# Reading and writing the columns of a matmul in other orders, in two feed-forward groups of a two-layer encoder

## The chip, the cores and the metric

The kernel runs on one core of a Trainium2 chip. The metric is the device time of one execution in microseconds. The kernel before takes 1174.57 us, the median of three runs (1173.69 to 1175.23).

## What is computed

Two layers act on x, 512 tokens by 1024 features. Each has an attention part (eight stick-breaking heads and four differential ones, with a common input and output projection) and a feed-forward part. In outline, with the attention left out:

```
for l in range(2):
    h = rmsnorm(x, attn_norm[l])
    x = x + attention(h @ w_in[l]) @ w_o[l]
    h = rmsnorm(x, mlp_norm[l])
    u = square(relu(h @ w_ff1[l]))      # 1024 -> 4096
    x = x + u @ w_ff2[l]                # 4096 -> 1024
return rmsnorm(x, final_norm)
```

The change lies in the product `h @ w_ff1[0]`.

## The kernel before

Activations lie transposed in SBUF: features on the 128 partitions, the 512 tokens along the free dimension. `h` has eight chunks of 128 features (`KC = 8`), held as two tiles, `h_hi` and `h_lo` ([128, 8, 512]): the value rounded to fp32r, and the remainder. Weights are split in the same way into `whi` and `wlo`, by one ScalarE copy (L116) and one VectorE subtraction (L117). A product is then three matmuls into the same PSUM bank, `hi x hi`, `hi x lo` and `lo x hi`; the helper `three` (L278) issues them at L281 to L283. In each the weight block of 128 x 128 is the stationary operand, and 512 columns of the other operand are the moving one. The output is one PSUM bank, 128 x 512 in fp32, so that column t of the moving operand gives column t of the bank.

The generator `block` (L291) computes 128 features of a projection for all tokens. It asks for a bank, takes the next weight unit, and issues `three` for each of the eight chunks in turn, 24 matmuls in all; the first opens the accumulation (`start`) and the last closes it (`stop`). `hpair(c)` gives the two halves of chunk c of `h`, `wpair(u, c)` those of the weights. Attention uses `block` for its projections, with names that begin with p; the feed-forward part uses it with names of the form `f{layer}_{group}_{k}`.

The feed-forward part works in four groups (`GROUPS = 4`), each of 1024 hidden features. A group has two halves. First come eight blocks (`2 * GP = 8`) of the first matrix. As each block ends, `evict_u` (L800) reads the bank: ScalarE takes the relu (L810) and squares it (L811), and sums and differences of the results are split into the tiles `Ah` and `Al` (L224, L225). Then the second matrix is multiplied in seven combinations of its quarters (`FORMS`, seven products in place of eight), which also go through `three`; their banks are gathered into `y` by ScalarE (L833) or VectorE (L835).

No order is written out by hand around the change: the framework places the instructions of each engine, and their order follows the program text. The weight unit after the next is split while the present one is used (`next`, L142), and while a group is computed its quarters of the second matrix are loaded and summed by DMA (`grow`, L783). In attention the projections are interleaved with scores (L465, L466), transposes of the attention weights (L555) and products with v (L583, L584; 256 columns each) by a budget of costs; this happens before the feed-forward part of the layer and has no bearing on the order within it. The v tiles are written by ScalarE at L381, in one of two layouts: for one head group in pieces of 64 columns, for the other in pieces of 128.

Of the kernel before, what the change touches and what calls it, by code (L numbers as in the profile page):

```python
# [22 lines left out]
KC = D // P  # L23
# [62 lines left out]
class _Weights:  # L86
# [55 lines left out]
    def next(self, kind):  # L142
        i = self.used
        assert _UNITS[i][0] in kind
        self.used += 1
        if i > 0:
            self.do_split(i + 2 * len(self.pools), i)
        return self.tiles.pop(i)
# [3 lines left out]
def trunk(ctx, tc, xT, w, w2, gains, gfin, lamv, cos, sin, out):  # L152
    nc = tc.nc
# [8 lines left out]
    def bank(tag, name):  # L162
        if tag == "any":
            tag = ("mm", "s", "s", "mm", "s")[turn[0] % 5]
            turn[0] += 1
        return ps.tile([P, 512], F32, tag=tag, name=name, bufs=banks[tag])
# [111 lines left out]
    def three(pt, a, b, first, last):  # L278
        ah, al = a
        bh, bl = b  # L280
        nc.tensor.matmul(pt, ah, bh, start=first, stop=False)  # L281
        nc.tensor.matmul(pt, ah, bl, start=False, stop=False)  # L282
        nc.tensor.matmul(pt, al, bh, start=False, stop=last)  # L283

    def hpair(c):
        return h_hi[:, c, :], h_lo[:, c, :]

    def wpair(u, c, n=P):
        return u[0][:, c * n : (c + 1) * n], u[1][:, c * n : (c + 1) * n]

    def block(name, tag="mm"):  # L291
        pt = bank(tag, name)
        u = W.next("px" if name[0] == "p" else "1")
        for c in range(KC):
            three(pt, wpair(u, c), hpair(c), c == 0, c == KC - 1)
            yield pt if c == KC - 1 else None

    def constants(a2):
# [18 lines left out]
    for l in range(L):  # L317
        with ExitStack() as actx:
# [379 lines left out]
            def dense():  # L698
                pts = opened_by.pop() if l else None
                if l == 0:  # L700
                    us = [W.next("x"), W.next("x")]
                    pts = [bank("mm", f"p{l}{i}") for i in range(2)]
                    turns = [(c, i) for c in range(5) for i in range(2)] + [(c, i) for i in range(2) for c in (5, 6, 7)]
                    for c, i in turns:
                        three(pts[i], wpair(us[i], c), hpair(c), c == 0, c == KC - 1)
                        yield 3 * 0.216
                step, b = 2 * KC, int(ORDER[0][1])
                held = [(pts[0], "d", b, "q"), (pts[1], "d", b, "k")]
                for item in ORDER[1:]:
                    kind, b = item[0], int(item[1])  # L710
                    for which in ("qk" if kind in "ds" else "v"):
                        name = f"p{l}{kind}{b}{which}"
                        for pt in block(name, "s" if step in (16, 24, 32) else "mm"):
                            step += 1
                            if step == RA[l]:
                                dgs["a"] = rms_a(ssq, 1.0 / D, rcol, f"a{l}", nc.vector, tr)
                            if step == RB[l]:
                                rms_b(rbc, f"a{l}", dgs["a"])
                                nc.vector.tensor_mul(cos_t, cos_t, rbc)
                                nc.vector.tensor_mul(sin_t, sin_t, rbc)  # L720
                            yield 3 * 0.216
                        held.append((pt, kind, b, which))
                        if step >= RB[l]:
                            for args in held:
                                {"w": evict_v, "u": evict_v, "s": evict_s, "d": evict_d}[args[1]](*args)
                            held = []
                yield from wo(1)
# [5 lines left out]
            for cost in dense():  # L733
# [5 lines left out]
                while live and credit > 0:  # L739
                    c = next(at, None)  # L740
# [17 lines left out]
        with ExitStack() as fctx:  # L758
            fp = fctx.enter_context(tc.tile_pool(name=f"ff{l}", bufs=1))
            f2 = fctx.enter_context(tc.tile_pool(name=f"f2{l}", bufs=2))  # L760
            last = l == L - 1
# [149 lines left out]
            for g in range(GROUPS):  # L911
# [12 lines left out]
                for k in range(2 * GP):  # L924
                    for n, pt in enumerate(block(f"f{l}_{g}_{k}", "any")):
                        if (g, k, n) == (0, 0, 6):
                            ptr = bank("t", f"rs_m{l}")
                            for j in range(4):
                                nc.tensor.transpose(ptr[:, j * P : (j + 1) * P], ssq[:, j * P : (j + 1) * P], ident)
                            nc.vector.tensor_reduce(  # L930
                                out=r2, in_=ptr.rearrange("p (j f) -> p j f", j=4), axis=AX.X, op=ALU.add)
                            nc.vector.tensor_scalar(
                                out=r2, in0=r2, scalar1=1.0 / D, scalar2=EPS, op0=ALU.mult, op1=ALU.add)
                            nc.vector.reciprocal(r2, r2)
                    evict_u(pt, g, k, forms)
                    if end and k in (2, 3):
                        settle(k - 2, 0)
                for f, form in enumerate(FORMS):
# [6 lines left out]
                    for n, (c, i, r) in enumerate(work):  # L945
                        if c not in held:
                            held[c] = W.next("f")
                        u = held[c]
# [65 lines left out]
            if last:  # L1014
                add_to(1, 0, to[1])
                square(1, 0)
                store(0, 0, False)
                weigh(0, 1)
                store(0, 1, True)
                weigh(1, 1, nc.gpsimd)  # L1020
                root(1)
                store(1, 0, False)
                store(1, 1, True)
            else:
                W.pools.pop()
                us = [W.next("x"), W.next("x")]
                pts = [bank("mm", f"p{l + 1}{i}") for i in range(2)]
                for tb in (0, 1):
                    add_to(tb, 0, to[tb])
                for c in CAME[2:4]:  # L1030
                    back(c)
                for n, c in enumerate(CAME):
                    if n in (2, 3):
                        for c_ in (CAME[4:6], CAME[6:])[n - 2]:
                            h = back(c_)
                    for i in range(2):
                        three(pts[i], wpair(us[i], c), hpair(c), n == 0, c == CAME[-1])
                squares = [add_sq(c, n == 0, ft, nc.vector) for n, c in enumerate(CAME)]
                for n in (0, 1):
                    behind(squares[n][n], h[n])  # L1040
                for p, q in zip(squares[1:], squares):
                    behind(p[0], q[0])
                opened_by.append(pts)
# [66 lines left out]
```

## Time and profile before

| | |
|---|---|
| median of three runs | 1174.57 us |
| span of the profiled execution | 1173.7 us |
| PE busy, share of the span | 1149.1 us, 98% |
| DVE busy, ACT busy | 817.8 us (70%), 651.7 us (56%) |
| share of PE in the chain that ended last | 84% |
| group 1 of layer 0, its eight blocks | 331.40 to 374.92 us |
| group 2 of layer 0, its eight blocks | 413.00 to 456.52 us |

The span is the time from the first to the last instruction of one profiled execution. PE is TensorE's matrix multiplication and PEld its weight loads, which run beside it; DVE is VectorE, ACT ScalarE, POOL GpSimd and SP the engine that issues most DMAs. In a row of the timeline stand the start, the duration (both in us), the engine, the line, the operation and its tiles, `out<-in`. `f` is the bank of a feed-forward block; names that begin with a number or `x`, such as `11010`, are banks of the seven combinations. A row of waits reads: who waited, for whom, us in total, how often, the longest.

### The profile page before, as it was taken

The numbers are of one execution on the slowest core, as the hardware profiler recorded it, in microseconds if no ns is written. First come the engines' busy times: TensorE is split into PE (matmuls) and PEld (weight loads), VectorE is DVE, ScalarE is ACT, GpSimd is POOL, SyncE is SP. The second block draws the span as 40 slices with busy tenths as digits, with TensorE's granted clock in tenths as the row PEclk, the third lists the DMA queues.
The fourth block names the chain that finished last, engine by engine and source line by source line (L and its number), as shares of the span: only waits on it lengthen the run. The fifth ranks groups of instructions, "written<-read, shape, count | busy, mean of one in ns | idle before, by whom it ended". The sixth has DMA issues, their size and how long they took to land.

```text
span 1173.7 us, 15335 instructions
## 1 busy us (share of the span) xinstructions
PE 1149.1 (98%) x5454; PEld 952.0 (81%) x5454; DVE 817.8 (70%) x1301; ACT 651.7 (56%) x1153; POOL 213.7 (18%) x283
## 2 busy tenths in 40 slices
PE   9999999999999999999899999999999999999995
PEld 6887888888888888888677888888888888888884
DVE  7888788785546747646878887877665466476567
ACT  6455666556656456455445556655666563554545
POOL 1221442130101101002012215331201010010022
PEclk9999999999999999999999999999999999999999
DMA  7645433245844836737416553432558357276184
GB/s 245 174 138 170 127 108 111 70 179 163 210 139 113 220 126 125 223 94 160 100 55 189 153 161 108 129 105 72 220 122 231 122 124 222 97 172 192 33 170 129
DMA packets 56860, 170.11 MB, mean 145 GB/s; under 512 B 7120, under 2 KB 8144, under 8 KB 56784
## 3 DMA queue, kind: packets, MB, share of 16 engines
q1 hardware_dynamic: 46416, 131.88, 33.7%
q0 software_dynamic: 10224, 37.23, 17.9%
q8 instruction: 43, 0.70, 0.2%
q14 instruction: 33, 0.27, 0.1%
q10 hardware_dynamic: 144, 0.02, 0.0%
HBM read 138.17 MB, written 2.10 MB: 120 GB/s over the span
## 4 chain that ended last, share of the span: by engine, by line
PE 84%; DVE 6%; DMA 3%; issue 2%; ACT 1%; POOL 1%; SPq 0%; POOLq 0%; DVEq 0%; ACTq 0%
PE f L282 10%; PE f L281 10%; PE f L283 10%; PE x L282 4%; PE x L281 4%; PE x L283 4%; PE wo L281 2%; PE wo L282 2%; PE wo L283 2%; DMA q<-in_w 2%; DVE wlo L117 1%; PE T0s L555 1%; PE T1s L555 1%; ACT whi L116 1%; DVE h_lo L229 1%
## 5 line engine op out<-in xcount | busy, mean ns | idle before, releaser
L117 DVE TENSOR_TENSOR wlo<-raw,whi 128x1024 fp32r<-128x1024 f32 (+1 forms) x132 | 158.0, 1201 | 95.9 <-ACT whi L116 95.0
L117 DVE TENSOR_TENSOR wlo<-q,whi 128x512 fp32r<-128x512 f32 x224 | 146.2, 688 | 106.0 <-ACT whi L116 105.6
L281 PE MATMUL f<-h_hi,whi 128*128 128x512 f32 x512 | 199.6, 390 | 0.0
L283 PE MATMUL f<-h_hi,wlo 128*128 128x512 f32 x512 | 199.2, 389 | 0.0
L282 PE MATMUL f<-h_lo,whi 128*128 128x512 f32 x512 | 199.2, 389 | 0.0
L116 ACT ACTIVATE whi<-q 128x512 fp32r<-128x512 f32 x224 | 129.5, 624 | 120.1 <-DMA q<-in_w 39.1
L116 ACT ACTIVATE whi<-raw 128x1024 fp32r<-128x1024 f32 (+1 forms) x132 | 133.9, 1019 | 111.0 <-PE f L282 54.5
L783 POOL DMA_DIRECT2D q<-in_w x64 | 55.9, 873 | 556.8 <-DVE wlo L117 471.4
L283 PEld LDWEIGHTS f<-h_hi,wlo 128*128 128x128 f32 x512 | 96.1, 188 | 20.0
L281 PEld LDWEIGHTS f<-h_hi,whi 128*128 128x128 f32 x512 | 96.1, 188 | 19.9
L282 PEld LDWEIGHTS f<-h_lo,whi 128*128 128x128 f32 x512 | 96.1, 188 | 19.7
L225 DVE TENSOR_TENSOR Al<-F,Ah 128x256 fp32r<-128x256 f32 (+2 forms) x96 | 74.8, 779 | 44.1 <-ACT Ah L224 44.0
L281 PE MATMUL x<-whi,Ah 128*128 128x512 f32 x256 | 100.2, 392 | 0.0
L282 PE MATMUL x<-wlo,Ah 128*128 128x512 f32 x256 | 99.7, 390 | 0.0
L283 PE MATMUL x<-whi,Al 128*128 128x512 f32 x256 | 99.7, 389 | 0.0
L224 ACT ACTIVATE Ah<-F 128x256 fp32r<-128x256 f32 (+2 forms) x96 | 67.6, 704 | 45.7 <-DVE F L819 43.7
L282 PEld LDWEIGHTS x<-wlo,Ah 128*128 128x128 f32 x256 | 48.1, 188 | 10.0 <-DVE wlo L117 0.4
L283 PEld LDWEIGHTS x<-whi,Al 128*128 128x128 f32 x256 | 48.0, 188 | 10.0
L281 PEld LDWEIGHTS x<-whi,Ah 128*128 128x128 f32 x256 | 48.1, 188 | 9.8
L810 ACT ACTIVATE F<-f 128x512 f32<-128x512 f32 x64 | 37.5, 587 | 9.9 <-DVE Al L225 5.5
L811 ACT ACTIVATE F<-F 128x512 f32<-128x512 f32 x64 | 40.3, 630 | 1.5
L228 ACT ACTIVATE h_hi<-x,g_all 128x512 fp32r<-128x512 f32 x32 | 22.6, 720 | 30.6 <-DVE x L692 17.5
(1060 smaller groups left out, 2574.6 us busy)
## 6 DMA issues: line engine op xcount, KB each, us to landing
raw<-in_w SPq DMA_DIRECT2D x126, 512.0 KB, 3.6
q<-in_w SPq DMA_DIRECT2D x64, 512.0 KB, 5.3
q<-in_w POOLq DMA_DIRECT2D x64, 512.0 KB, 5.7
x<-in_xT SPq DMA_DIRECT2D x8, 256.0 KB, 4.1
raw<-in_w SPq DMA_DIRECT2D x8, 128.0 KB, 4.1
yx<-y POOLq DMA_DIRECT2D x2, 512.0 KB, 8.8
y<-y POOLq DMA_DIRECT2D x2, 512.0 KB, 7.5
y<-yx POOLq DMA_DIRECT2D x2, 512.0 KB, 5.2
```

What stands on the lines that cost most here:

```text
L116: h = nc.scalar.activation(hi[:, a:b], raw[:, a:b], AF.Copy)
L117: self.last = h, nc.vector.tensor_tensor(out=lo[:, a:b], in0=raw[:, a:b], in1=hi[:, a:b].bitcast(F32), op=ALU.subtract)
L224: nc.scalar.activation(hi, src, AF.Copy)
L225: nc.vector.tensor_tensor(out=lo, in0=src, in1=hi.bitcast(F32), op=ALU.subtract)
L228: a = nc.scalar.activation(h_hi[:, c, :], x[:, c, :], AF.Copy, scale=g)
L281: nc.tensor.matmul(pt, ah, bh, start=first, stop=False)
L282: nc.tensor.matmul(pt, ah, bl, start=False, stop=False)
L283: nc.tensor.matmul(pt, al, bh, start=False, stop=last)
L555: nc.tensor.transpose(pt[:, off : off + P], u["w"][qi][:, kb * P : (kb + 1) * P], ident)
L783: nc.gpsimd.dma_start(t, quad(g, q, c), accum_op=ALU.add)
L810: nc.scalar.activation(t, pt, AF.Relu)
L811: nc.scalar.activation(t, t, AF.Square)
```

## The change

A table `READS` names an order for each of the eight chunks. `None` is the plain order, columns 0 to 511. A pair (n, b) cuts the 512 columns into n equal streams and takes b neighbouring columns of each stream in turn: with (2, 16) columns 0 to 15, 256 to 271, 16 to 31, 272 to 287, and so on. The same rearranged view is put on the moving operand and on the PSUM bank, so that each column's result lands where it did before. `three_by` is `three` with that view. `block` calls it for every projection, but with an order other than the plain one only where the name begins with `f0_1` or `f0_2`: groups 1 and 2 of layer 0, eight blocks each. The second matrix, attention and all other groups keep the plain order. Later lines move down by 17.

```
--- before.py
+++ after.py
@@ -282,6 +282,23 @@
         nc.tensor.matmul(pt, ah, bl, start=False, stop=False)
         nc.tensor.matmul(pt, al, bh, start=False, stop=last)
 
+    READS = (None, (2, 16), (2, 8), (2, 4), (2, 32), (4, 16), (2, 2), (8, 16))
+
+    def turns(c):
+        def view(t):
+            if READS[c] is None:
+                return t
+            n, b = READS[c]
+            return t.rearrange("p (n a b) -> p a n b", n=n, b=b)
+        return view
+
+    def three_by(pt, a, b, first, last, view):
+        ah, al = a
+        bh, bl = b
+        nc.tensor.matmul(view(pt), ah, view(bh), start=first, stop=False)
+        nc.tensor.matmul(view(pt), ah, view(bl), start=False, stop=False)
+        nc.tensor.matmul(view(pt), al, view(bh), start=False, stop=last)
+
     def hpair(c):
         return h_hi[:, c, :], h_lo[:, c, :]
 
@@ -292,7 +309,7 @@
         pt = bank(tag, name)
         u = W.next("px" if name[0] == "p" else "1")
         for c in range(KC):
-            three(pt, wpair(u, c), hpair(c), c == 0, c == KC - 1)
+            three_by(pt, wpair(u, c), hpair(c), c == 0, c == KC - 1, turns(c if name[:4] in ("f0_1", "f0_2") else 0))
             yield pt if c == KC - 1 else None
```

## The prediction

> **What bounds the kernel now.** I read the profile page first, its busy shares and its chain of waits.
>
> ```profile
> span 1173.7 us, 15335 instructions
> ## 1 busy us (share of the span) xinstructions
> PE 1149.1 (98%) x5454; PEld 952.0 (81%) x5454; DVE 817.8 (70%) x1301; ACT 651.7 (56%) x1153; POOL 213.7 (18%) x283
> ...
> PE 84%; DVE 6%; DMA 3%; issue 2%; ACT 1%; POOL 1%; SPq 0%; POOLq 0%; DVEq 0%; ACTq 0%
> PE f L282 10%; PE f L281 10%; PE f L283 10%; PE x L282 4%; PE x L281 4%; PE x L283 4%; PE wo L281 2%; PE wo L282 2%; PE wo L283 2%; DMA q<-in_w 2%; DVE wlo L117 1%; PE T0s L555 1%; PE T1s L555 1%; ACT whi L116 1%; DVE h_lo L229 1%
> ```
>
> TensorE carries 84% of the chain, and the three matmul lines that the change touches head the list. A 98% busy PE need not run at its best rate, so the stretches in question decide. From the timeline of PE I took where the two edited groups begin and end, and asked for the busy time of each engine in those two stretches and the one between them; first the f matmuls alone, then everything.
>
> ```profile
> 331.40:374.92 43.52, 43.52 (x192) 35.85 (x191) 4.11 (x7) 1.00 0.39 111
> 413.00:456.52 43.52, 43.52 (x192) 35.85 (x191) 4.10 (x7) 1.00 0.38 110
> ```
> ```profile
> 331.40:374.92 43.52, 43.52 (x193) 36.04 (x192) 21.26 (x30) 24.08 (x38) 1.73 (x2) 1.00 0.39 111
> 413.00:456.52 43.52, 43.52 (x193) 36.04 (x192) 22.25 (x32) 23.49 (x36) 1.72 (x2) 1.00 0.38 110
> ```
>
> The columns are the stretch, PE, weight loads, then (second fence) DVE, ACT and POOL, the granted clock, the DMA share and GB/s. In each stretch 192 matmuls fill 43.52 us without a gap: 43.52 / 192 = 226.7 ns from one start to the next. The clock is granted in full, 1.00. The timeline at the end of the first stretch shows the same beat one by one: three steps from 374.24 to 374.92 are 0.68 us.
>
> ```profile
> 374.24 0.39 PE L281 MATMUL f<-h_hi,whi 128*128 128x512 f32 x1
> 374.47 0.39 PE L282 MATMUL f<-h_lo,whi 128*128 128x512 f32 x1
> 374.70 0.39 PE L283 MATMUL f<-h_hi,wlo 128*128 128x512 f32 x1
> 374.92 0.39 PE L281 MATMUL 11010_3748<-whi,Ah 128*128 128x512 f32 x1
> ```
>
> The 0.39 us is the record of one matmul, with a modelled end; consecutive ones overlap, so the price of a matmul is the 226.7 ns between starts. Last, the waits between 331 and 457 us. Thirteen rows came back, and none begins with PE:
>
> ```profile
> POOL q L783 <- DVE wlo L117: 114.8, 7, 46.0
> DVE wlo L117 <- ACT whi L116: 40.4, 22, 4.0
> ACT whi L116 <- PE f L282: 27.4, 10, 4.2
> ...
> POOL q L783 <- issue: 0.2, 1, 0.2
> ```
>
> So PE never waits in this region, while ACT waits for PE. DVE (21 to 22 us of 43.52) and ACT (24 us) are about half idle. Whatever a reordered matmul costs or saves is paid one for one in the end time: there is no PE gap to hide it, and none that it could close.
>
> **The change part by part.** Nothing is removed, added or moved: 192 + 192 matmuls, the same weights, the same 512 columns, the same banks, the same buffers, DMAs and waits. What differs is the order in which 7 of the 8 chunks walk the columns. Each of the 16 blocks has three matmuls a chunk, so each order is run by 16 x 3 = 48 matmuls and the seven orders by 336; chunk 0 keeps its order. A walk is cut into runs of b neighbouring columns: 512 / b of them, that is 32, 64, 128, 16, 32, 256 and 32 for chunks 1 to 7, 560 in all, so 48 x 560 = 26,880 runs where there were 336.
>
> *The matmul itself.* No PE instruction of this trace reads or writes in pieces, so I bound the cost. Below: how much of the 226.7 ns does not grow with the columns? The 256-column matmuls tell.
>
> ```profile
> 207.74 0.28 PE L583 MATMUL O0s<-fh0s,vs 128*128 128x256 f32 x1
> 207.85 0.28 PE L584 MATMUL O0s<-fl0s,vs 128*128 128x256 f32 x1
> 207.97 0.28 PE L583 MATMUL O0s<-fh0s,vs 128*128 128x256 f32 x1
> 208.09 0.28 PE L584 MATMUL O0s<-fl0s,vs 128*128 128x256 f32 x1
> 208.21 0.40 PE L281 MATMUL wo<-mdh,whi 128*128 128x512 f32 x1
> ```
>
> Four steps from 207.74 to 208.21 are 0.47 us, 117.5 ns each. A column is (226.7 - 117.5) / 256 = 0.427 ns, so 512 of them are 218.4 ns and 8.3 ns are left over for each matmul. Every matmul pays the per-column part; an order could save at most the 8.3 ns. That is the lower end: 336 x 8.3 ns = 2.8 us gained.
>
> Above: the slowest column rate of a warm PE in this trace is that of the transposes.
>
> ```profile
> 205.79 0.49 PE L555 MATMUL T0s<-edge,sig0s 128*128 128x128 f32 x3
> ```
> ```profile
> L555 PE MATMUL T0s<-edge,sig0s x80: 270/272/301, 134.6 to 220.3; 128*128 128x128 f32 x80
> ```
>
> Three of them take 0.49 us to the last one's end, and one alone has a record of 0.27, so the two steps are 0.22 us: about 109 ns for 128 columns, 0.85 ns a column. A 512-column matmul at that rate would be 435 ns, 208 ns more than now. Taking it as the upper end, the cost of one order is between -0.4 us and 48 x 0.208 = 10.0 us, and of all seven between -2.8 us and 69.9 us.
>
> Between ends so far apart I go by the nearest row with a cut-up access. ScalarE has it: L381 writes the v tiles of one attention group as eight runs of 64 columns, those of the other as four runs of 128, and L224 writes `fh` in one run of 512, all from a PSUM bank.
>
> ```profile
> L381 ACT ACTIVATE vs<-vT0u x4: 597/602/610, 120.1 to 197.2; 128x512 fp32r<-128x512 f32 x4
> ```
> ```profile
> L381 ACT ACTIVATE vdh<-vT0w x4: 578/598/599, 37.6 to 94.7; 128x512 fp32r<-128x512 f32 x4
> ```
> ```profile
> L224 ACT ACTIVATE fh0s<-T0s x8: 597/600/607, 146.3 to 220.0; 128x512 fp32r<-128x512 f32 x8
> ```
>
> 602, 598 and 600 ns: a jump at the end of a run costs that engine nothing that can be seen. It is another engine, at a slower column rate and on the SBUF side; but it is an address walk of the same kind, and I take 0 for the matmul too. Both ends stay for the range.
>
> *Partial sums.* All three matmuls of a chunk use one order and each element is still added to once per matmul. From one chunk to the next the orders differ, so an element can come up again after fewer than 512 columns. Laying the walks end to end, the shortest return is 162 columns, from chunk 6 to chunk 7, or 162 x 0.427 = 69 ns; at all other borders it is 258 or more. In the rows above, 256-column matmuls of one accumulation return to an element every 117.5 ns without a stall; 69 ns is not shown. It would concern one border a block, 16 in all, and even 208 ns at each are 3.3 us; I price it at 0.
>
> *Weight loads and readers.* Each weight load has to fit beside a matmul: 35.85 / 191 = 188 ns of 226.7, so 39 ns are free and reordered matmuls can only lengthen that cover. ACT reads a bank when the last matmul of its block has ended, in its old order; its tile and its wait are the same.
>
> Sum: 1173.7 us of span plus 0. The three timed runs have a median of 1174.57 (1173.69 to 1175.23), 0.9 above the span of the profiled execution, so I forecast 1174.6. About 0.2%, 2.3 us, is what a measurement of this kernel can tell from no change.
>
> The rows cannot say how the memories that PE reads and writes treat a run of a given length. [...]
>
> **The rivals.**
>
> *Only the shortest runs cost.* Chunk 6 walks two streams in runs of two. Its reads change place 256 times a matmul, twice as often as chunk 3's. If the memory behind PE delivers in pieces longer than two columns, PE waits in chunk 6 alone. Price: at the transposes' rate 48 x 0.208 = 10.0 us, 1184.6: slower, against my forecast. It decides the verdict from 2.3 us / 48 = 48 ns a matmul. For it: each column now has only 0.427 ns, so there is no room for a second access. Against it: seven orders, and only one so short. 0.16.
>
> *Every run end costs.* If the address walk loses one column's time at each end of a run, in any order, that is 26,880 x 0.427 ns = 11.5 us, 1186.1; at two columns' time 1197.6. For it: PE walks a column in 0.427 ns where ScalarE takes 600 / 512 = 1.17 ns, fixed cost included, so it has less time to turn. Against it: the ScalarE rows, where seven further run ends cost 2 ns. 0.12, of which a little over half for one column's time.
>
> *Any order but the plain one is slow.* All 336 at the transposes' rate: 69.9 us, 1244.5. For it: no matmul of this trace is cut up, so no row excludes it. [...]
>
> *Faster.* Were the 8.3 ns a conflict between a matmul's first columns and the one before it, another order could dissolve it: at most 2.8 us, 1171.8. Against it: every matmul, in any order, still starts at column 0 and ends at 511, where a conflict between neighbours would lie. 0.03.
>
> **How the numbers follow.** The four rivals hold 0.40 and scatter and others 0.03. No change has 0.57. Slower by over 0.2%: 0.16 + 0.12 + 0.09 and 0.02 of the rest, 0.39. Faster by over 0.2%: 0.04. Predicted is the likeliest, 1174.6. The range goes from 1171.8, all 8.3 ns saved, to 1187.0, just past the short-run case and one column's time per run end: 0.57 + 0.16 + 0.07 + 0.02, about 0.82. Not in it are slow matmuls in all orders and run ends of two columns' time or more.
>
> **What would show it.** The two stretches of 192 f matmuls should again be 43.52 us; layer 1 has the same groups in the plain order and is the measure beside them. Within a block the 24 starts should be 226.7 ns apart throughout. If steps 19 to 21 of each block alone are longer, the first rival holds; if the excess goes as 32, 64, 128, 16, 32, 256, 32, the second; if chunks 1 to 7 are all long and alike, the third; steps of 218 ns would be the fourth. I am wrong if the two stretches differ from 43.52 by more than 1.2 us each, and wrong in kind if the time shows up elsewhere, such as a wait of PE within the region.

## The result, and the profile after

The changed kernel takes 1183.03 us, the median of three runs (1182.60 to 1186.01), against 1174.57 before: a ratio of 1.0079 with a 95% interval of 1.0057 to 1.0100. It is slower by 8.5 us. The forecast was no change; the range held the time, and what the likeliest case said of the matmuls was wrong.

The page of the changed kernel, in the parts shown of the one before:

```profile
span 1184.2 us, 15335 instructions
## 1 busy us (share of the span) xinstructions
PE 1159.4 (98%) x5454; PEld 953.4 (81%) x5454; DVE 818.3 (69%) x1301; ACT 652.1 (55%) x1153; POOL 214.1 (18%) x283
...
PE 84%; DVE 6%; issue 2%; DMA 2%; ACT 2%; POOL 1%; SPq 0%; POOLq 0%; ACTq 0%; DVEq 0%
```

The instructions are as many as before on every engine. PE is busy for 10.3 us more, and the span is 10.5 us longer; the other engines do the same work. Where the time lies is seen in the two stretches of 192 f matmuls (columns: stretch, PE, weight loads, ACT, granted clock, DMA share, GB/s):

```profile
331.82:380.12 48.30, 48.30 (x192) 36.31 (x191) 4.06 (x7) 1.00 0.38 102
418.22:466.52 48.30, 48.30 (x192) 36.31 (x191) 4.06 (x7) 1.00 0.36 98
```

Each is 48.30 us where it was 43.52: 4.78 us more, 9.6 us together, at the same clock. The profiled run was the slowest of the three, and the 0.9 us by which the span differs further lie inside the 3.4 us by which these runs differ. The waits between 331 and 467 us still have no row that begins with PE:

```profile
POOL q L800 <- DVE wlo L117: 123.7, 8, 48.4
DVE wlo L117 <- ACT whi L116: 48.2, 24, 4.6
ACT whi L116 <- PE f L299: 38.6, 16, 4.7
...
ACT whi L116 <- PE 11011_3749 L283: 0.2, 1, 0.2
```

The others wait longer for PE (ACT 38.6 us where it was 27.4, in a window 10 us longer); the time is inside the matmuls. The timeline of PE shows which. These are chunks 5, 6 and 7 of one block, and the first matmul of the next:

```profile
353.52 0.40 PE L298 MATMUL f<-h_hi,whi 128*128 128x512 f32 x1
353.76 0.40 PE L299 MATMUL f<-h_lo,whi 128*128 128x512 f32 x1
353.99 0.40 PE L300 MATMUL f<-h_hi,wlo 128*128 128x512 f32 x1
354.23 0.51 PE L298 MATMUL f<-h_hi,whi 128*128 128x512 f32 x1
354.56 0.51 PE L299 MATMUL f<-h_lo,whi 128*128 128x512 f32 x1
354.90 0.51 PE L300 MATMUL f<-h_hi,wlo 128*128 128x512 f32 x1
355.24 0.41 PE L298 MATMUL f<-h_hi,whi 128*128 128x512 f32 x1
355.49 0.40 PE L299 MATMUL f<-h_lo,whi 128*128 128x512 f32 x1
355.72 0.40 PE L300 MATMUL f<-h_hi,wlo 128*128 128x512 f32 x1
355.96 0.40 PE L298 MATMUL f<-h_hi,whi 128*128 128x512 f32 x1
```

The three starts from 354.23 to 355.24, chunk 6, take 1.01 us, 337 ns each. Chunk 5 takes 0.71 us, 237 each, and chunk 7 0.72, 240 each; all were 227. Over the 16 blocks, from start to start, the mean of each chunk is:

| chunk | 0 | 1 | 2 | 3 | 4 | 5 | 6 | 7 |
|---|---|---|---|---|---|---|---|---|
| order | plain | (2,16) | (2,8) | (2,4) | (2,32) | (4,16) | (2,2) | (8,16) |
| ns a matmul | 231.6 | 240.3 | 241.7 | 250.7 | 236.3 | 234.7 | 337.3 | 240.0 |
| above 226.7 | 4.9 | 13.6 | 15.0 | 24.0 | 9.6 | 8.0 | 110.6 | 13.3 |

Each order has 48 matmuls, and the excesses add up to 199.0 ns, so this is 48 x 199.0 ns = 9.6 us, of which chunk 6 has 5.3 and the others 4.2. Group 3 of layer 0 and groups 1 and 2 of layer 1, in plain order, keep 43.52 us.

### The profile page after: what moved, and what is told of

Same layout as the page of the kernel before. It is cut to its first block, busy times and chain, and to the rows that moved or that the text cites. A ratio compares the mean times of both kernels' runs of the same rounds, so it can differ in the third digit from the quotient of the medians.

```text
span 1184.2 us, 15335 instructions
## 1 busy us (share of the span) xinstructions
PE 1159.4 (98%) x5454; PEld 953.4 (81%) x5454; DVE 818.3 (69%) x1301; ACT 652.1 (55%) x1153; POOL 214.1 (18%) x283
## 4 chain that ended last, share of the span: by engine, by line
PE 84%; DVE 6%; issue 2%; DMA 2%; ACT 2%; POOL 1%; SPq 0%; POOLq 0%; ACTq 0%; DVEq 0%
PE f L298 10%; PE f L300 10%; PE f L299 10%; PE x L283 4%; PE x L282 4%; PE x L281 4%; PE wo L281 2%; PE wo L283 2%; PE wo L282 2%; DVE wlo L117 2%; PE T1s L572 1%; PE T0s L572 1%; DMA q<-in_w 1%; ACT whi L116 1%; DVE h_lo L229 1%
## 5 line engine op out<-in xcount | busy, mean ns | idle before, releaser
L298 PE MATMUL f<-h_hi,whi 128*128 128x512 f32 x512 | 203.2, 397 | 0.0
L300 PE MATMUL f<-h_hi,wlo 128*128 128x512 f32 x512 | 202.6, 396 | 0.0
L299 PE MATMUL f<-h_lo,whi 128*128 128x512 f32 x512 | 202.6, 396 | 0.0
L282 PEld LDWEIGHTS x<-wlo,Ah 128*128 128x128 f32 x256 | 48.1, 188 | 10.3 <-DVE wlo L117 0.5
```

Of the source, the lines that this page charges most:

```text
L298: nc.tensor.matmul(view(pt), ah, view(bh), start=first, stop=False)
L299: nc.tensor.matmul(view(pt), ah, view(bl), start=False, stop=False)
L300: nc.tensor.matmul(view(pt), al, view(bh), start=False, stop=last)
```

## The experiments

Two questions were put to the chip. On which side does an order cost, where the operand is read or where the bank is written? And what of an order sets the cost: the length of a run, its place in memory, or the jump? Most kernels give each of the eight blocks of a group one order for all its 24 matmuls, so that one window of the profile, divided by 24, is the price of one order. Four kernels were run several times for their time; the others ran once.

**One order a block, on both sides.** The view is chosen by the block's number in place of the chunk's:

```
+    def pick(name):
+        return int(name[5]) if name[:4] in ("f0_1", "f0_2") else 0
...
-            three_by(pt, wpair(u, c), hpair(c), c == 0, c == KC - 1, turns(c if name[:4] in ("f0_1", "f0_2") else 0))
+            three_by(pt, wpair(u, c), hpair(c), c == 0, c == KC - 1, turns(pick(name)))
```

> The eight orders are kept, but each of the eight blocks of a group uses one of them for all its 24 matmuls (block 0 the plain one, block 6 runs of two columns), on the operand and on the bank as before. What is read is the step from start to start in the middle of a block. Theory 1, the cost belongs to the order itself: the steps are those of the changed kernel, 337 ns for runs of two, 251 for runs of four, 235 to 242 for the longer runs, and 227 in block 0; the two stretches come to about 48.2 us each. Theory 2, the small excess of 8 to 14 ns comes from going from one order to another at each chunk: inside a block the runs of 8 columns and more go back to 227, and a stretch is about 24 x (110 + 24) ns = 3.2 us above 43.52, so 46.7 us.

Windows of group 1 by block, f matmuls on PE: block 0 (plain), block 1, (2,16), and block 6 (runs of two). A window can count a neighbour's tail as a 25th or 26th matmul; its width is what counts.

```profile
330.77:336.21 5.44, 5.44 (x24) 1.00 0.61 193
336.21:341.97 5.76, 5.76 (x25) 1.00 0.35 118
...
365.08:373.09 8.01, 8.01 (x26) 1.00 0.62 110
```

The plain block has 5.44 / 24 = 226.7 ns and the block with runs of two 8.01 / 24 = 333.8. All eight come to 226.7, 240.0, 243.3, 250.8, 236.7, 231.8, 333.8 and 239.2, 48.06 us a stretch (1182.41 us in one run, before 1174.29). Theory 1 holds: the cost is the order's own, and going from one order to the next adds little (48.30 us a stretch with an order for each chunk).

**The operand alone.** `view` is taken off the bank in `three_by`, and ScalarE puts the columns back:

```
-        nc.tensor.matmul(view(pt), ah, view(bh), start=first, stop=False)
+        nc.tensor.matmul(pt, ah, view(bh), start=first, stop=False)
...
-            nc.scalar.activation(t, pt, AF.Relu)
+            nc.scalar.activation(turns(pick(f"f{l}_{g}_{k}"))(t), pt, AF.Relu)
```

> One order a block, on the moving operand alone; the bank is written in plain order and ScalarE puts the columns back when it reads the bank. Theory 1, the cost sits where the operand is read: 337 ns a step with runs of two, the small excess at the longer runs too, 48 us a stretch. Theory 2, it sits where the bank is written: 227 ns in all eight blocks and 43.5 us a stretch. If both sides cost, some of the 110 ns shows here and the rest in the kernel that reorders the bank alone.

Blocks 0, 3 (runs of four) and 6:

```profile
331.82:337.26 5.44, 5.44 (x24) 1.00 0.59 194
...
348.86:354.88 6.02, 6.02 (x25) 1.00 0.27 88
...
366.13:374.14 8.01, 8.01 (x26) 1.00 0.66 114
```

Block for block the same widths as with both sides: 6.02 / 24 = 250.8 ns, 8.01 / 24 = 333.8. The whole cost is where the operand is read (1183.79 us in one run).

**The bank alone.** The mirror image: `view(pt)` stays, `view(bh)` and `view(bl)` go, and ScalarE reads `view(pt)`.

> One order a block, on the PSUM bank alone; the operand is read in plain order and ScalarE reads the bank in the order in which it was written. Theory 1, the cost sits where the operand is read: 227 ns in all blocks, 43.5 us a stretch. Theory 2, it sits where the bank is written (and added to): 337 ns with runs of two, 48 us a stretch.

```profile
330.37:335.81 5.44, 5.44 (x25) 1.00 0.55 185
...
363.01:368.45 5.44, 5.44 (x26) 1.00 0.54 96
```

All sixteen blocks, that with runs of two among them, take 5.44 us. In these eight orders, what PE writes and adds to a bank costs nothing extra. The same kernel timed:

> The kernel that reorders the bank alone, one order a block, timed. Theory 1, the order of writing is free in PE and ScalarE's reads in pieces are off the path: no difference from before, within 0.05%. Theory 2, the run before had a gain elsewhere that hid a cost: the time is above before by 1 us or more.

1175.08 us, ratio 1.0001 (0.9992 to 1.0010): no difference. Bank patterns in runs of two columns and more leave a matmul at 226.7 ns in all eight orders.

**More orders.** Both sides, sixteen orders, the first eight for the blocks of group 1 and the others for those of group 2 (1208.73 us in one run, before 1174.29).

```
+    READS = (None, (2, 128), (2, 64), (4, 8), (4, 4), (8, 4), (4, 2), (8, 2), (16, 2), (64, 4), (128, 2), (32, 8), (32, 2), (64, 2), (16, 8), (16, 4))
...
+        return int(name[5]) + 8 * (name[3] == "2") if name[:4] in ("f0_1", "f0_2") else 0
```

> One order a block on both sides, and sixteen orders instead of eight: in group 1 plain, (2,128), (2,64), (4,8), (4,4), (8,4), (4,2), (8,2), in group 2 (16,2), (64,4), (128,2), (32,8), (32,2), (64,2), (16,8), (16,4). Theory 1, the length of a run decides: all six orders with runs of two take about 337 ns a step, all four with runs of four about 250, the others 235 to 242, whatever the number of streams. Theory 2, the distance of the jump or the number of streams decides: runs of two differ among themselves by tens of ns, and (128,2), whose jumps skip only two columns, is far below 337. Theory 3, each run end costs about one column's time, 0.43 ns: 337 for runs of two, 281 for four, 254 for eight, 241 for sixteen, 230 for 64 and 128.

Six windows, in order (2,128), (2,64), (4,4), (4,2), (64,4), (128,2):

```profile
335.89:341.33 5.44, 5.44 (x25) 1.00 0.33 118
341.33:346.77 5.44, 5.44 (x25) 1.00 0.29 96
...
352.31:358.73 6.42, 6.42 (x25) 1.00 0.27 82
...
365.42:376.09 10.67, 10.67 (x25) 1.00 0.35 58
...
436.74:442.35 5.61, 5.61 (x25) 1.00 0.28 93
442.35:453.16 10.81, 10.81 (x25) 1.00 0.16 49
```

Runs of 64 and 128 columns cost nothing, 226.7 ns. Runs of four are 233.8 ns with 64 streams, 267.5 with four and 278 with eight; runs of two are 445 to 450 with four and 128 streams, and 432 to 487 with the numbers between. The 334 of two streams is the exception among runs of two, not their price. (128,2) reads columns 0, 1, 4, 5, 8, 9 and so on: its jumps skip two columns, and yet it takes 450 ns, while (64,4) with half as many run ends takes 234. So neither the number of run ends (theory 3) nor the length of the jump (theory 2) sets the time. Theory 1 is right that the length decides above all, and wrong in its numbers. The windows of these two orders suggest something sharper: the time goes with the visits to aligned blocks of four columns, 16 bytes. (64,4) goes to 128 of them once, like the plain order; (128,2) goes to the same 128 twice. That is 128 more visits in 450.4 - 226.7 ns, by estimate 1.75 ns each.

**The operand two columns later.** If visits to blocks of four are what is paid for, runs of four that start in the middle of a block must cost like runs of two. The tiles `h_hi` and `h_lo` were made four columns longer, and begin 8 bytes later (1230.03 us in one run, before 1175.36):

```
-    h_hi = cp.tile([P, KC, S], F32R, tag="h_hi", name="h_hi")
...
+        cp.tile([P, KC * S + 4], F32R, tag=n, name=n)[:, 2 : 2 + KC * S].rearrange("p (c s) -> p c s", c=KC)
```

> The two tiles of h begin 8 bytes (two columns) later, so that a run of four columns no longer starts where a block of four columns (16 bytes) starts. Both groups, one order a block on both sides: plain, (2,64), (2,4), (64,4), (2,8), (32,8), (2,2), (128,2) in group 1; (2,16), (2,32), (4,16), (8,16), (4,4), (16,8), (4,8), (8,2) in group 2. Theory 1, PE fetches aligned blocks of four columns at about 1.7 ns each ((450 - 13) ns over 256 blocks in the order (128,2)), and what a run touches is counted in blocks: a run of b columns now touches b/4 + 1 of them. Runs of four then take 256 blocks, about 440 ns, where they took 234 to 267; runs of eight 192 blocks, about 335; of sixteen 160, about 280; of thirty-two 144, about 255; of sixty-four 136, about 240; plain 129, 228. Runs of two still touch one block each and stay at 334 for (2,2), 450 for (128,2), 487 for (8,2). Theory 2, the length of the run alone decides: every order keeps its time to within some ns, (64,4) at 234, (32,8) at 233.

Windows in order (2,64), (2,4), (64,4), (32,8), (128,2):

```profile
339.43:345.48 6.05, 6.05 (x25) 1.00 0.30 98
345.48:353.44 7.96, 7.96 (x25) 1.00 0.20 66
353.44:364.31 10.87, 10.87 (x25) 1.00 0.15 50
...
372.74:380.77 8.03, 8.03 (x25) 1.00 0.40 65
...
388.88:399.76 10.88, 10.88 (x25) 1.00 0.47 95
```

(64,4) goes from 233.8 to 452.9 ns, the price of (128,2), which stays at 453.3. (32,8) goes from 233.1 to 334.6 (expected 335), the three orders with runs of sixteen to 284 to 293 (280), (2,32) to 262.0 (255), (2,64) to 252.1 (240). Runs of two stay near their times: 338.0 for (2,2) and 493.6 for (8,2). So the visits to blocks set most of the time, and the length of a run matters mainly through them. Theory 2 falls. The misses: the other runs of eight are at 351 to 359 and (4,4) at 474, each 15 to 35 ns above what the count gives; (2,4) is 331.7 in place of 440, again the case of two streams that each take a block in two halves with one run of the other stream between, as in (2,2); and even the plain order is 234.6 in place of 228, and not in the edited groups alone:

```profile
543.47:588.49 45.02, 45.02 (x192) 36.41 (x191) 4.12 (x7) 1.00 0.40 107
```

This is group 3, plain before and after, 45.02 us for 43.52.

**The weight load reading one place.** Orders of whole blocks with runs below 64 columns, 231 to 278 ns, still cost 4 to 52 ns above 226.7. The next matmul's weight load runs beside the present matmul (36.31 / 191 = 190 ns of each step in a changed stretch). Does the place that it reads get in the way?

```
+    def weights(name, u, c):
+        if name[:4] in ("f0_1", "f0_2"):
+            return (ones_r.to_broadcast([P, P]),) * 2
+        return wpair(u, c)
```

> In groups 1 and 2 of layer 0 every matmul takes one constant column of ones, repeated 128 times, as its stationary operand instead of the weights, so the weight load reads one place in SBUF instead of 128 columns; the products with those weights are left out, and the output is another. One order a block: the eight of the changed kernel in group 1; (8,4), (4,4), (16,4), (4,2), (8,2), (128,2), (64,4), (2,64) in group 2. Theory 1, the small excess over 227 ns (13 ns for (2,16), 10 for (2,32), 24 for (2,4), 40 for (4,4), 52 for (8,4)) comes from the weight load of the next matmul reading SBUF beside the moving operand: all orders with whole blocks of four columns fall to 227 or close to it, and runs of two keep 334 and 450. Theory 2, it comes from the moving operand's own walk: every order keeps its time to within 2 ns.

Group 1's blocks 0 (plain) and 1, (2,16):

```profile
331.00:336.56 5.56, 5.56 (x25) 1.00 0.63 198
336.56:342.32 5.76, 5.76 (x26) 1.00 0.87 233
```

(2,16) stays at 240.0 ns, (4,4) at 268.8, (8,4) at 275.9. Theory 1 falls: the excess stays when the weight load reads one column in place of 128. Nor does DMA traffic set it: (2,16) has the same 5.76 us at a DMA share of 0.35 in the first kernel of this section and of 0.87 here. Theory 2 isn't clean either: (8,16) comes down from 239.2 to 233.6 and (2,32) from 236.7 to 233.6, while the plain order and (2,64) go up to 231.7 and 231.5. A few ns come and go with this edit; most of the excess does not. A weight load still runs beside each matmul (191 of them, 36.17 us, in group 1's stretch), so what its reading costs at all is not shown.

**The parts, timed.** Chunk 6 put back in plain order:

```
-    READS = (None, (2, 16), (2, 8), (2, 4), (2, 32), (4, 16), (2, 2), (8, 16))
+    READS = (None, (2, 16), (2, 8), (2, 4), (2, 32), (4, 16), None, (8, 16))
```

> The changed kernel with chunk 6, the runs of two columns, put back in plain order; the other six orders stay, one a chunk. Theory 1, both the short runs and the jumps of the longer ones cost: of the 9.6 us found in the two stretches chunk 6 has 48 x 110.6 ns = 5.3 us, so 4.2 us are left, a ratio of about 1.0036. Theory 2, my first rival as it was put, only the shortest runs cost: no difference from before, within 0.05%.

1178.28 us against 1174.98 (23 runs), ratio 1.0029 (1.0018 to 1.0040), that is 2.1 to 4.7 us. A stretch of this kernel:

```profile
331.24:376.89 45.65, 45.65 (x192) 36.06 (x191) 4.12 (x7) 1.00 0.40 107
```

45.65 - 43.52 = 2.13, twice 4.3 us. The first rival as it was put, with a cost in chunk 6 alone, falls.

Chunk 6 alone reordered, `READS = (None,) * 6 + ((2, 2), None)`:

> Only chunk 6 reads and writes in runs of two columns; all other chunks are plain. Theory 1: 48 matmuls by about 107 to 111 ns, 5.1 to 5.3 us, a ratio of about 1.0045, and the plain chunks on either side keep 227 ns or lose a few ns at the border. If the borders between orders were what costs, the plain chunk behind it would show tens of ns.

1180.93 us, ratio 1.0056 (1.0042 to 1.0069), 4.9 to 8.1 us.

```profile
330.42:376.81 46.39, 46.39 (x192) 36.07 (x191) 4.08 (x7) 1.00 0.38 106
```

2.87 us a stretch, 5.7 together. Chunk 6 takes 334 ns; the plain chunk behind it takes 236 and the plain one after that 229.6, where both were 226.7. So some ns of a slow chunk appear in the two plain ones behind it.

Runs of 64 and 128 by turns in all seven chunks:

> Chunks 1 to 7 in two streams with runs of 64 and 128 columns by turns, on both sides. Theory 1, jumps that come after 64 columns or more are free (226.7 ns a step when a whole block used one such order): no difference from before, within 0.05%, and 43.5 us a stretch. Theory 2, every matmul with a rearranged view pays some fixed time, or going from one order to another costs: 5 to 10 ns for each of 336 matmuls, 1.7 to 3.4 us.

1174.27 us, ratio 0.9999 (0.9988 to 1.0009); both stretches are 43.52 us:

```profile
330.48:374.00 43.52, 43.52 (x192) 35.85 (x191) 4.11 (x7) 1.00 0.41 111
```

With runs this long, neither a rearranged view nor a change of order costs anything in itself. No kernel of the four that were run several times was faster than the one before.

## Why the prediction was right or wrong

- *PE is the bound there, and what a matmul gains or loses is paid one for one:* right. The stretches grew by 9.6 us and the timed ratio allows 6.7 to 11.7. Each stretch differs from 43.52 by 4.78 us, and the prediction had named 1.2 us as the sign that it is wrong.
- *The cost of an order is 0:* wrong, and this is the step that failed. It rested on ScalarE's 602 and 598 ns for writes in eight and four pieces against 600 in one. Those rows had no run below 64 columns, and runs of 64 columns are free on PE too (226.7 ns). They said nothing about short runs, where a visit uses only half of a block, nor about PE, for which four columns are 4 x 0.427 = 1.71 ns and one further visit was paid with about as much, by estimate 1.75 ns. The measured mean over the seven orders is (9.6 us - 0.2 of chunk 0) / 336 = 28 ns. Over half of the 9.6 us, 5.3, is chunk 6, which takes each block in two halves; the rest comes almost all with runs of 4 to 32 columns, and its cause is open.
- *The bounds, -0.4 to 10.0 us an order:* they held. Chunk 6 had 5.3 us; the dearest order tried, (8,2), takes 487 ns, 12.5 us for 48 matmuls, outside them.
- *Partial sums, weight loads, readers at 0:* right. Orders on the bank alone are free (5.44 us a block), and chunk 7, behind the closest return, takes 240.0 ns in the changed kernel and 239.2 where a whole block has its order. A weight load in the changed stretches takes 36.31 / 191 = 190 ns, still inside a step.
- *Only the shortest runs cost (1184.6):* closest in total, by two errors that nearly cancel: chunk 6 cost 5.3 us and not 10.0, and the other chunks 4.2 and not 0.
- *Every run end costs:* 0.427 ns a run end gives 109 ns for chunk 6 and 13.7 for chunk 1, and 110.6 and 13.6 were measured; but it gives 54.7 for chunk 3, where 24.0 was measured. The agreement was chance: (64,4) pays 7 ns for 128 run ends and (128,2) 224 for 256.
- *Any order but the plain one is slow (1244.5, chance 0.09):* wrong on both sides; runs of 64 are free to read and all runs tried on the bank alone are free to write, 226.7 ns each.
- *Faster:* no order went below 226.7 ns.
- *The range, 1171.8 to 1187.0:* it held the time by luck. Its upper end came from two rivals, and none of the patterns of steps that the prediction named (chunk 6 alone, an excess that goes as the run ends, all seven alike) is the one in the table.

Open remain two things. Why whole blocks in jumps of less than 64 columns cost 4 to 52 ns, in no order of streams or distances (four-column runs: 250.8 with 2 streams, 267.5 with 4, 278.4 with 8, 247.2 with 16, 233.8 with 64), is not settled; the place that the weight load reads was ruled out as the main cause. And why two streams that take each block in two halves pay for about half of the second visits (334 ns, 61 further visits of 1.75 ns in place of 128) was not tried.

## What to carry to other kernels

When a rearranged moving operand is planned for fp32r matmuls, count how often it goes to an aligned 16-byte block, as the times here went with that for the most part ((64,4) took 233.8 ns, and 452.9 when moved by 8 bytes): 128 times for 512 columns is the least. The orders in runs of two that go to each block twice took 432 to 487 ns, that is (432.4 - 226.7) / 128 = 1.6 ns to (487.2 - 226.7) / 128 = 2.0 ns for each further visit, and about half of that with two streams. Keep runs at 64 columns or more (226.7 ns), as whole blocks in shorter runs still cost 4 to 52 ns a matmul, or put the rearrangement on the PSUM side, which was free down to runs of two (226.7 ns). A zero taken from another engine's row holds only for the sizes that the row has.

## What the runs showed of the hardware

The start of the moving operand matters even when it is read in order: with `h` begun 8 bytes later each plain matmul of group 3 took 234.5 ns and not 226.7, 3.4%. And ScalarE reads a bank in these orders as fast as in plain order: its 64 reads of f banks, 14 of them in other orders, took 576 ns at least, 579 in the median and 601 at most, both in the kernel that reorders the bank alone and before. Where it wrote SBUF in these orders, in the kernel that reorders the operand alone, seven such instructions in a stretch came to 4.15 us in both groups, against 4.11 and 4.10 before; as seven plain ones came to 4.19 in the kernel with the constant weights, those 0.04 us are no firm price.
